# Where a one-number tile lies, and where all tiles behind it begin

## The chip, the core and the metric

The kernel runs on one core of one Trainium2 chip. Five engines work side by side: TensorE (PE in the profile, with its weight loads listed as PEld), VectorE (DVE), ScalarE (ACT), GpSimd (POOL) and SyncE (SP), which only starts transfers. The metric is the device time of one execution in microseconds. Three runs of the kernel before took 1090.83, 1091.79 and 1092.25 us; the median is 1091.79 us.

## The reference

One decoder block for 512 tokens of width 1024, in float32:

```
h     = rms_norm(x)
uv, z, xBC, dt, gates = split(h @ w_in)
y_a   = gelu(u) * (W_s @ layer_norm(gelu(v)) + b)     in 128-token chunks, W_s lower triangular
y_b   = rms_norm(ssd_scan(silu(conv(xBC)), dt) * silu(z))      32 heads, 8 groups, chunks of 128
x     = x + (sigmoid(ga) * (y_a @ w_proj_a) + sigmoid(gb) * (y_b @ w_proj_b)) @ w_out
x     = x + relu(rms_norm(x) @ w_mlp_up)**2 @ w_mlp_down
out   = rms_norm(x)
```

Nearly all of the arithmetic lies in the large products h @ w_in, the three projections and the two MLP products.

## The kernel before, in words

Every large product is made exact enough by splitting each factor in two parts of type float32r, a high part and the rest, and by adding three products: high by low, low by high, high by high. These are lines 132, 133 and 134 (`mm3`). TensorE takes two operands: a stationary one of 128 rows by 128 columns, which a weight load brings in, and a moving one of 128 rows and up to 512 columns, which streams past it. In the profile's names "acc<-hTl,whi" the moving operand is named first (hTl) and the stationary one second (whi).

The weights come as slabs of 128 x 1024 numbers. `Slabs` (lines 66 to 106) loads a slab from memory into `wraw`, ScalarE copies it into `whi`, and VectorE writes the rest to `wlo` (lines 91 and 92). Two orders of the product exist. `chan_major` (line 189) holds a weight part stationary and lets 512 tokens of the activations move past it: hT (the normalised input), yA, yB (the branches' outputs) and h2 (the second norm's output). `tok_major` (line 146) holds 128 tokens of the activations stationary and lets 512, or 352, weight columns move. The small products of the scan (lines 495, 573 to 575, 599, 601, 639) and the transposes (lines 225, 601, 658, against the unit matrix `ident`) are woven between the large ones by a list of due steps (`Weave`, line 111).

Order and waits come from the order of the code and from the tile framework. What matters here is where tiles lie. A pool is a stretch of each partition of the on-chip memory; pools opened on the left side follow one another in the order in which they are opened, and each tile in them begins at the next multiple of 32 bytes. The left side is opened as const, wpool, small, dtp, big, htp, and then pools that come and go behind these. One pool, mg, which holds the merged activations mh and ml of the output projection, is opened from the right end.

The tile in question is `mhalf` (line 285): the number -0.5 in each partition, 4 bytes, which POOL uses as the exponent of each inverse square root (lines 207, 473, 652). It lies in const, between `ident` and `triu`. Since it takes 32 bytes and not a multiple of 128, everything behind it starts 32 bytes past a multiple of 128; after the pool small, whose tiles add 1216 bytes, everything starts 96 past one.

Of the kernel before, what the change touches and what calls it, by code (L numbers as in the profile page):

```python
# [10 lines left out]
F32 = mybir.dt.float32  # L11
# [6 lines left out]
P = 128  # L18
T = 512
NT = T // P  # L20
DM = 1024
# [4 lines left out]
HD = 64  # L26
DFF = 4096
EPS = 1e-6
# steps (of three products of 512 columns) from a group's projection to the stages of its scan
SD, SA, SI, SS, SB, SC = 9, (12, 20), 8, 7, 9, 9  # L30
N2D = 8
WARM = 2, 0

# columns of the per-channel parameter tile
PV_CONVW, PV_CONVB, PV_BG, PV_SSMG = 0, 128, 160, 176
PV_N = 192
SL = 1024
# v's columns and dt's 32 go in three groups of 352, dt's first
VW = 352
NV = 12  # L40

# [2 lines left out]
def block_kernel(ctx: ExitStack, tc: tile.TileContext, x, w_v, w_all, wspt, pvec, hvec, g_mix, g_mlp, g_fin, v_g, v_b,  # L44
# [6 lines left out]
    const = ctx.enter_context(pool("const"))  # L51
# [10 lines left out]
    def sm_tile():  # L62
        return ps.tile([P, T], F32, tag="sm", name="sm", bufs=4)

# [1 line left out]
    class Slabs:  # L66
        def __init__(self):
            self.ready, self.raws, self.loaded, self.made = [], [], 0, 0
# [25 lines left out]
            self.made += 1  # L94

        def ahead(self, n):
            """Have n slabs in the making beyond those taken."""
            while len(self.ready) < n and self.made < self.n:
                self.make()

# [6 lines left out]

    slabs = Slabs()

# [1 line left out]
    class Weave:  # L111
        def __init__(self):
            self.now, self.due, self.seq = 0.0, [], 0
# [14 lines left out]
    wv = Weave()  # L128

    def mm3(o, st, mv, first, last, d=1.0):  # L130
        """o (+)= stationary.T @ moving, both as (hi, lo) parts"""
        nc.tensor.matmul(o, st[0], mv[1], start=first, stop=False)  # L132
        nc.tensor.matmul(o, st[1], mv[0], start=False, stop=False)  # L133
        nc.tensor.matmul(o, st[0], mv[0], start=False, stop=last)  # L134
        wv.step(d)
# [8 lines left out]
        return slice(t * P, (t + 1) * P)  # L144

    def tok_major(actT, evac, order="slabs", n=T, halve_last=False):
        """For n output columns: 4 token tiles, 4 slabs of two k-tiles with the weights moving."""
        accs = [acc_tile()[:, :n] for _ in range(NT)]

        def unit(t, kk, w):  # L150
            for j in range(2):
                k = 2 * kk + j
                mm3(accs[t], cut(actT, k, tsl(t)), wk(w, j, n), k == 0, k == KD - 1, n / T)

        if order == "slabs":
            for kk in range(4):
                w = slabs.take()
                for t in range(NT):
                    unit(t, kk, w)
                    if kk == 3:  # L160
                        evac(t, accs[t])
        else:
            # the last token tile by halves of the columns, for a shorter way out
            ws = [slabs.take(0)]
            last = [accs[-1][:, 0:256], sm_tile()[:, 0:256]] if halve_last else []

            def half(hf, kk):
                for j in range(2):
                    k = 2 * kk + j
                    w = cut(ws[kk], slice(j * T + hf * 256, j * T + (hf + 1) * 256))  # L170
                    mm3(last[hf], cut(actT, k, tsl(NT - 1)), w, k == 0, k == KD - 1, 0.5)

            slabs.ahead(2)
            for t in range(NT - len(last) // 2):
                unit(t, 0, ws[0])
            for hf in range(len(last)):
                half(hf, 0)
            ws += [slabs.take(0) for _ in range(3)]
            slabs.ahead(1)
            for t in range(NT - len(last) // 2):  # L180
                for kk in (1, 2, 3):
                    unit(t, kk, ws[kk])
                evac(t, accs[t])
            for hf in range(len(last)):
                for kk in (1, 2, 3):
                    half(hf, kk)
                evac(NT - 1, last[hf], hf)

    def chan_major(actT, evac, n=1, ahead=2):
        """n tiles of 128 output channels over all tokens, the weights stationary."""  # L190
        for i in range(n):
            w = slabs.take(ahead)
            acc = acc_tile()
            for k in range(KD):
                mm3(acc, wk(w, k), cut(actT, k), k == 0, k == KD - 1)
            evac(i, acc)

# [1 line left out]
    pv = const.tile([P, PV_N], F32, name="pv")  # L199
    hv = const.tile([P, 96], F32, name="hv")  # L200

    def rms_scale(ss):
        """(ss / DM + EPS) ** -0.5"""
        ms = small.tile([P, 1], F32, tag="rms_ms", name="rms_ms", bufs=4)
        nc.vector.tensor_scalar(ms, ss, 1.0 / DM, EPS, ALU.mult, ALU.add)  # L205
        rs = small.tile([P, 1], F32, tag="rms_rs", name="rms_rs", bufs=4)
        nc.gpsimd.tensor_tensor(rs, ms, mhalf, ALU.pow)  # L207
        return rs

    def rms_norm(xt, gs, work):  # L210
        """The 128 tokens of xt normalised over the free dim, times the gains gs (by halves)."""
        sq = work.tile([P, DM], F32, tag="rms_sq", name="rms_sq", bufs=1)
        ss = small.tile([P, 1], F32, tag="rms_ss", name="rms_ss", bufs=4)
        nc.scalar.activation(sq, xt, AF.Square, accum_out=ss)  # L214
        rs = rms_scale(ss)
        h = work.tile([P, DM], F32, tag="rms_h", name="rms_h", bufs=2)
        for b in range(2):
            hb = slice(b * T, (b + 1) * T)
            nc.vector.scalar_tensor_tensor(h[:, hb], xt[:, hb], rs, gs[b], ALU.mult, ALU.mult)  # L219
        return h  # L220
# [30 lines left out]
    gm = gm_cm.__enter__()  # L251
    v = gm.tile([P, NT, DM], F32, name="v")

# [1 line left out]
    ph0_cm = pool("ph0")  # L255
    ph0 = ph0_cm.__enter__()
    grow = ph0.tile([1, DM], F32, name="grow")
# [2 lines left out]
    with tc.manual_schedule():  # L260
# [11 lines left out]
        for i in range(2):  # L272
            for b in range(2):
# [8 lines left out]
        ident = const.tile([P, P], F32, name="ident")  # L282
        nc.gpsimd.affine_select(ident, ones, pattern=[[-1, P]], base=0, channel_multiplier=1,
                                compare_op=ALU.is_equal, fill=0.0)
        mhalf = const.tile([P, 1], F32, name="mhalf")
        nc.gpsimd.memset(mhalf, -0.5)
        # triu[s, l] = 1 where s <= l
        triu = const.tile([P, P], F32, name="triu")
        nc.gpsimd.affine_select(triu, ones, pattern=[[1, P]], base=0, channel_multiplier=-1,
                                compare_op=ALU.is_ge, fill=0.0)  # L290
# [32 lines left out]
            hs.append(h)  # L323

        def part(i, b, eng):
            """half a slab into its parts, the low one by eng"""
            if eng is None:
                nc.scalar.copy(parts[i][0][:, b], raws[i][:, b])
            else:
                eng.tensor_sub(parts[i][1][:, b], raws[i][:, b], parts[i][0][:, b].bitcast(F32))  # L330
# [69 lines left out]
                nc.scalar.activation(v[:, t, 0:VW - NH], accs[t][:, NH:VW], AF.Gelu)  # L400
                nc.vector.tensor_add(xr[:, t, :], accs[t][:, 0:NH], hv[:, 0:NH])

# [1 line left out]
    def dt_side():  # L404
        def softplus():
            # softplus(x) = max(x, 0) + log1p(exp(-|x|)); log1p(e) = 2 atanh(e / (2 + e))
            xf = flat(xr)
            ax, e, d, u, u2, q = (dtw.tile([P, NC], F32, name=f"dt_{i}") for i in range(6))
            nc.vector.scalar_tensor_tensor(ax, xf, -1.0, xf, ALU.mult, ALU.max)
# [38 lines left out]

    dt_side()

# [1 line left out]
    gm2_cm = pool("gm2")  # L452
    gm2 = gm2_cm.__enter__()
    wsp = gm2.tile([P, NG, P], F32, name="wsp")
# [61 lines left out]
    chan_major(yA, pa_evac, KD)  # L516
    ya_cm.__exit__(None, None, None)

# [1 line left out]
    ybp_cm = pool("ybp")  # L520
    ybp = ybp_cm.__enter__()
    yB = tuple(ybp.tile([P, KD, T], F32R, name=n) for n in ("yBh", "yBl"))
# [27 lines left out]
        return xc  # L550

    def ssd(g, xc, last_delay=None):
        """Weave the group's scan into the steps to come."""
        h0, h1 = R * g, R * (g + 1)
        st = {}

# [18 lines left out]
            nc.tensor.matmul(o, a[0], b[0], start=False, stop=True)  # L575

        def decay(hf):
            """exp(cs[l] - cs[s]) of two chunks, where s <= l"""
            lm = sd.tile([P, 2, R, P], F32, tag="lm", name="lm", bufs=2)
            for j in range(2):  # L580
                nc.sync.dma_start(lm[:, j], csd[2 * hf + j, h0:h1, :].partition_broadcast(P))
            lmf = lm.rearrange("p j r q -> p (j r q)")
            for j in range(2):
                for r in range(R):
                    nc.vector.tensor_scalar(lm[:, j, r, :], lm[:, j, r, :], ncs[:, 2 * hf + j, h0 + r:h0 + r + 1], None,
                                            ALU.add)
                st["lm", 2 * hf + j] = lm[:, j]
            nc.gpsimd.affine_select(lm, lm, pattern=[[0, 2], [0, R], [1, P]], base=0, channel_multiplier=-1,
                                    compare_op=ALU.is_ge, fill=-1e30)
            nc.scalar.activation(lmf, lmf, AF.Exp)  # L590
# [26 lines left out]
            st[c] = lm, xdt, xD  # L617

        def stage_s(c):
            """the state after chunk c"""  # L620
            hs = st.get("hs")
            stp = sm_tile()
            mm3s(stp[:, 0:256], *st["s", c])
# [60 lines left out]
        if g == 4:  # L684
            chan_major(yB, pb1_evac, KD)

# [1 line left out]
    def gb_evac(n, acc):  # L688
        sg = sd.tile([P, T], F32, tag="cv", name="sgb", bufs=2)
        nc.scalar.activation(sg, acc, AF.Sigmoid, bias=pv[:, PV_BG + KD + n:PV_BG + KD + n + 1])  # L690
# [30 lines left out]
    ybp_cm.__exit__(None, None, None)  # L721
    ht_cm.__exit__(None, None, None)
    tok_major(mg_t, res_evac(0))
    # the second half leads into the second norm, token tile by token tile
    n2 = ctx.enter_context(pool("n2"))
    gbc = n2.tile([P, DM], F32, name="gbc2")
    nc.sync.dma_start(gbc, g_mlp.partition_broadcast(P))
# [10 lines left out]

    mg_cm.__exit__(None, None, None)

# [1 line left out]
    mp_cm = pool("mlp")  # L742
    mp = mp_cm.__enter__()
    for qd in range(4):
# [57 lines left out]
    mp_cm.__exit__(None, None, None)  # L802


# [1 line left out]
def _stationary(w):  # L806
    """[K, N] -> [N / 128, 128 (k in tile), K]: one slab for 128 outputs over K = 1024"""
    k, n = w.shape
    return w.reshape(k // P, P, n // P, P).transpose(2, 1, 0, 3).reshape(n // P, P, k)


def _moving(w):
    """[K, N] -> [N / 512, K / 256, 128 (k in tile), 1024]: slabs of two k-tiles for 512 outputs"""
    k, n = w.shape
    return w.reshape(k // 256, 2, P, n // T, T).transpose(3, 0, 2, 1, 4).reshape(n // T, k // 256, P, SL)

# [52 lines left out]
```

## Time and profile before

| what | value |
|---|---|
| median of three runs | 1091.79 us |
| the profiled execution, first to last instruction (span) | 1088.7 us |
| PE busy, and its loads (PEld) | 1076.5 us (99%), 896.0 us (82%) |
| DVE, ACT, POOL busy | 612.6, 439.3, 137.3 us |
| mean granted TensorE clock | 0.998 |

The runs' times hold about 3 us that lie around the span. A PE at 99% is always at work by this measure, but the measure doesn't tell at what pace: the profile models the ends of matmuls, and one lasts longer than the distance from its start to the next start. The pace is read from the starts.

### The profile page before, as it was taken

To read this page: it belongs to the slowest core of one execution; us is meant where nothing else is said; L and a number is where in the kernel's file an instruction comes from. 1 tells how busy PE (TensorE), PEld (TensorE's weight loads), DVE (VectorE), ACT (ScalarE), POOL (GpSimd) and SP (SyncE) were. 2 spreads that over 40 slices of the span, in tenths; PEclk is the share of its full clock that TensorE was granted. 3 is DMA by queue.
4 is the path that set the end of the run, shared out by engine and by line. 5 is a ranking of instruction groups with operands and counts; after the bars stand their busy time and mean duration, and the time that the engine had idled before them with its cause. 6 is when DMAs were issued, how large, how long until landed. Compare 5 with 4: busy or idle time off the path is not lost. (4 is left out here: it accounts for less than half of the span.)

```text
span 1088.7 us, 13415 instructions
## 1 busy us (share of the span) xinstructions
PE 1076.5 (99%) x5205; PEld 896.0 (82%) x5205; DVE 612.6 (56%) x1040; ACT 439.3 (40%) x666; POOL 137.3 (13%) x188
## 2 busy tenths in 40 slices
PE   8999999999999999999999999999999999999997
PEld 7988888888888888888887888889888888888886
DVE  4672444346887895647778865364344434433443
ACT  5643333334556456444565532244213313312332
POOL 3020000001432432301324300000000000000000
PEclk9999999999999999999999999999999999999999
DMA  6433224232333333332323233513233232233222
GB/s 210 140 124 102 78 80 135 96 97 78 98 98 116 98 97 116 98 97 93 101 78 98 78 97 115 195 61 115 97 97 96 93 95 86 95 97 97 97 78 78
DMA packets 34626, 111.32 MB, mean 102 GB/s; under 512 B 3970, under 2 KB 4738, under 8 KB 34563
## 3 DMA queue, kind: packets, MB, share of 16 engines
q1 hardware_dynamic: 34560, 110.46, 31.9%
q8 instruction: 41, 0.67, 0.2%
q14 instruction: 23, 0.18, 0.1%
q10 hardware_dynamic: 2, 0.00, 0.0%
HBM read 108.29 MB, written 2.16 MB: 101 GB/s over the span
## 5 line engine op out<-in xcount | busy, mean ns | idle before, releaser
L92 DVE TENSOR_TENSOR wlo<-wraw,whi 128x1024 fp32r<-128x1024 f32 (+1 forms) x178 | 214.9, 1208 | 179.5 <-ACT whi L91 179.3
L91 ACT CAST whi<-wraw 128x1024 fp32r<-128x1024 f32 (+1 forms) x178 | 183.2, 1030 | 227.8 <-PE acc L134 210.8
L132 PE MATMUL acc<-hTl,whi 128*128 128x512 f32 x448 | 181.8, 406 | 0.0
L133 PE MATMUL acc<-hTh,wlo 128*128 128x512 f32 x448 | 176.9, 395 | 0.0
L134 PE MATMUL acc<-hTh,whi 128*128 128x512 f32 x448 | 176.8, 395 | 0.0
L132 PE MATMUL acc<-h2l,whi 128*128 128x512 f32 (+1 forms) x288 | 106.6, 370 | 0.2 <-DVE h2l L229 0.2
L134 PE MATMUL acc<-h2h,whi 128*128 128x512 f32 (+1 forms) x288 | 106.3, 369 | 0.0
L133 PE MATMUL acc<-h2h,wlo 128*128 128x512 f32 (+1 forms) x288 | 106.3, 369 | 0.0
L134 PEld LDWEIGHTS acc<-hTh,whi 128*128 128x128 f32 x448 | 84.0, 188 | 20.5
L134 PE MATMUL acc<-whi,ah 128*128 128x512 f32 (+1 forms) x256 | 99.9, 390 | 0.0
L133 PE MATMUL acc<-whi,al 128*128 128x512 f32 (+1 forms) x256 | 99.4, 388 | 0.0
L132 PE MATMUL acc<-wlo,ah 128*128 128x512 f32 (+1 forms) x256 | 98.5, 385 | 0.0
L132 PEld LDWEIGHTS acc<-hTl,whi 128*128 128x128 f32 x448 | 84.3, 188 | 17.1
L133 PEld LDWEIGHTS acc<-hTh,wlo 128*128 128x128 f32 x448 | 84.3, 188 | 17.1
L545 DVE SCALAR_TENSOR_TENSOR cv<-acc,pv,cv 128x511 f32<-128x511 f32 (+2 forms) x96 | 71.5, 745 | 31.8 <-ACT cv L543 31.1
L132 PE MATMUL acc<-wlo,hTh 128*128 128x512 f32 (+1 forms) x208 | 78.0, 375 | 0.1
L133 PE MATMUL acc<-whi,hTl 128*128 128x512 f32 (+1 forms) x208 | 76.0, 366 | 0.0
L134 PE MATMUL acc<-whi,hTh 128*128 128x512 f32 (+1 forms) x208 | 75.8, 366 | 0.0
L750 DVE TENSOR_TENSOR relu<-relu 128x512 f32<-128x512 f32 x32 | 22.2, 693 | 89.8 <-ACT relu L749 89.8
L207 POOL TENSOR_TENSOR rms_rs<-rms_ms,mhalf 128x1 f32<-128x1 f32 x12 | 6.6, 550 | 458.4 <-DVE rms_ms L205 458.4
L749 ACT ACTIVATE relu<-acc 128x512 f32<-128x512 f32 x32 | 19.2, 599 | 111.5 <-PE acc L134 111.5
L132 PEld LDWEIGHTS acc<-h2l,whi 128*128 128x128 f32 x288 | 54.1, 188 | 10.7 <-DVE h2l L229 0.6
(202 smaller groups left out, 1848.9 us busy)
## 6 DMA issues: line engine op xcount, KB each, us to landing
wraw<-in_w_all SPq DMA_DIRECT2D x168, 512.0 KB, 3.5
lm<-csd SPq DMA_DIRECT2D x32, 256.0 KB, 4.3
wraw<-in_w_v SPq DMA_DIRECT2D x10, 352.0 KB, 3.3
x<-in_x SPq DMA_DIRECT2D x4, 512.0 KB, 5.4
out<-rms_h SPq DMA_DIRECT2D x8, 256.0 KB, 2.1
xt<-in_x SPq DMA_DIRECT2D x3, 512.0 KB, 6.2
wraw<-in_w_v SPq DMA_DIRECT2D x4, 176.0 KB, 5.3
xt<-in_x SPq DMA_DIRECT2D x2, 256.0 KB, 3.3
```

The source lines that it names most:

```text
L91: nc.scalar.copy(hi, raw)
L92: nc.vector.tensor_sub(lo, raw, hi.bitcast(F32))
L132: nc.tensor.matmul(o, st[0], mv[1], start=first, stop=False)
L133: nc.tensor.matmul(o, st[1], mv[0], start=False, stop=False)
L134: nc.tensor.matmul(o, st[0], mv[0], start=False, stop=last)
L207: nc.gpsimd.tensor_tensor(rs, ms, mhalf, ALU.pow)
L545: nc.vector.scalar_tensor_tensor(cv[:, s_:], acc[:, :T - s_], cw[:, 3 - s_:4 - s_], cv[:, s_:], ALU.mult, ALU.add)
L749: nc.scalar.activation(r_, acc, AF.Relu)
L750: nc.vector.tensor_mul(r_, r_, r_)
```

## The change

`mhalf` leaves const for small, where it is given 16 numbers (64 bytes) of which the first is used. All other edits are removed comments and shifted line numbers. As built, the instructions of each engine, their order and their waits are the same as before; only addresses differ.

```diff
-        mhalf = const.tile([P, 1], F32, name="mhalf")
+
+        mhalf = small.tile([P, 16], F32, name="mhalf")[:, 0:1]
         nc.gpsimd.memset(mhalf, -0.5)
```

In the built programs the tiles that TensorE reads begin at these distances past a multiple of 128 bytes (a slice of such a tile starts at a multiple of 128 from the tile's own start):

| tiles | role | before | after |
|---|---|---|---|
| ident, ones | both roles in small products | 0 | 0 |
| triu | stationary, one product | 32 | 0 |
| whi, wlo | stationary in chan_major, moving in tok_major | 32 | 0 |
| hT, yA, yB, h2 (high and low) | moving in chan_major, hT stationary in tok_major too | 96 | 0 |
| ah, al (the MLP's activations) | stationary in tok_major | 96 | 0 |
| v, wsp, xc, lm, xdt, bT, cT, xdd2, hs2, yg, rms_h | the small products | 96 | 0 |
| mh, ml | stationary in the output projection | 96 | 96 |

## Rows read from the trace of the kernel before

**Rows 1.** The page, part 1: busy time, share of the span, instructions.
```profile
span 1088.7 us, 13415 instructions
PE 1076.5 (99%) x5205; PEld 896.0 (82%) x5205; DVE 612.6 (56%) x1040; ACT 439.3 (40%) x666; POOL 137.3 (13%) x188
```

**Rows 2.** Waits of PE: engine, line, waited for, us in total, times, longest.
```profile
PE sm L658 <- DVE yg L653: 2.3, 2, 1.8
PE acc L296 <- POOL mhalf L286: 1.4, 1, 1.4
PE sm L225 <- DVE rms_h L322: 1.3, 2, 1.0
```

**Rows 3.** Groups of PE's matmuls by shape: count, busy us, mean ns, idle before.
```profile
L132 PE MATMUL acc<-hTl,whi 128*128 128x512 f32 x448 | 181.8, 406 | 0.0
...
L132 PE MATMUL acc<-wlo,ah 128*128 128x512 f32 x248 | 96.3, 388 | 0.0
...
L132 PE MATMUL acc<-h2l,whi 128*128 128x512 f32 x224 | 88.6, 395 | 0.0
...
L132 PE MATMUL acc<-wlo,hTh 128*128 128x512 f32 x128 | 52.1, 407 | 0.1
L132 PE MATMUL acc<-yBl,whi 128*128 128x512 f32 x128 | 51.3, 401 | 0.0
...
L132 PE MATMUL acc<-wlo,hTh 128*128 128x352 f32 x80 | 25.9, 324 | 0.0
...
L132 PE MATMUL acc<-wlo,mh 128*128 128x512 f32 x64 | 25.3, 395 | 0.0
L132 PE MATMUL acc<-yal,whi 128*128 128x512 f32 x64 | 25.2, 394 | 0.0
...
L132 PE MATMUL acc<-h2l,whi 128*128 128x256 f32 x64 | 18.0, 281 | 0.2 <-DVE h2l L229 0.2
```

**Rows 4.** PE in order of time, chan_major at 816 us: start us, us, what.
```profile
816.00 0.39 PE L134 MATMUL acc<-h2h,whi 128*128 128x512 f32 x1
...
818.80 0.39 PE L134 MATMUL acc<-h2h,whi 128*128 128x512 f32 x1
```

**Rows 5.** The same view, tok_major at 776 us.
```profile
775.71 0.39 PE L132 MATMUL acc<-wlo,ah 128*128 128x512 f32 x1
...
778.46 0.39 PE L132 MATMUL acc<-wlo,ah 128*128 128x512 f32 x1
```

**Rows 6.** The same view, 352 columns at 40 us.
```profile
39.76 0.32 PE L134 MATMUL acc<-whi,hTh 128*128 128x352 f32 x1
...
43.12 0.32 PE L134 MATMUL acc<-whi,hTh 128*128 128x352 f32 x1
```

**Rows 7.** The same view: transposes against ident, and 256-column products, at 729 to 735 us.
```profile
728.79 0.28 PE L132 MATMUL acc<-h2l,whi 128*128 128x256 f32 x1
...
730.91 0.28 PE L132 MATMUL acc<-h2l,whi 128*128 128x256 f32 x1
...
731.97 1.04 PE L225 MATMUL sm<-ident,rms_h 128*128 128x128 f32 x8
...
733.20 0.28 PE L132 MATMUL acc<-h2l,whi 128*128 128x256 f32 x1
...
734.56 0.28 PE L132 MATMUL acc<-h2l,whi 128*128 128x256 f32 x1
```

**Rows 8.** The same view, small products whose operands both lie 96 past.
```profile
306.09 0.28 PE L573 MATMUL sm<-xdd2l,bTh 128*128 128x256 f32 x1
...
306.45 0.40 PE L132 MATMUL acc<-wlo,hTh 128*128 128x512 f32 x1
```

**Rows 9.** Busy time by stretch: engines, granted clock, DMA share, GB/s.
```profile
560.00:640.00 80.00, 78.25 (x413) 65.72 (x413) 68.47 (x141) 40.32 (x71) 26.65 (x35) 1.00 0.28 81
730.00:1088.00 358.00, 351.93 (x1635) 290.65 (x1633) 147.03 (x181) 106.43 (x149) 2.19 (x4) 1.00 0.30 95
```

**Rows 10.** POOL's inverse square roots, which read mhalf: duration min/median/max, first and last.
```profile
L207 POOL TENSOR_TENSOR rms_rs<-rms_ms,mhalf x12: 548/550/557, 6.0 to 1083.8; 128x1 f32<-128x1 f32 x12
```

## The prediction

> **What bounds the kernel now.** I read the busy shares first, then TensorE's waits, then its groups by shape, and then single starts in order of time. The shares show PE busy for 1076.5 of 1088.7 us, with the next engine at 56% [rows 1]. The waits show that PE stands still for somebody else during 2.3 + 1.4 + 1.3 us [rows 2], and 0.2 us more before h2's first product [rows 3]: 5.2 us in all. So there is no wait to take away: the time is the number of products times the distance between their starts, and only that distance can change it much. It has to be read from starts, since the modelled duration of a 512-column product (388 to 407 ns, [rows 3]) overlaps its successor.
>
> The distances: with activations moving, twelve 512-column products take from 816.00 to 818.80 us, 233.3 ns each [rows 4]. With weights moving, twelve take from 775.71 to 778.46 us, 229.2 ns each [rows 5]. With 352 columns, 21 products (seven rounds of three) take from 39.76 to 43.12 us, 160.0 ns each [rows 6]. The granted clock is 1.00 from 730 us on [rows 9] and 0.998 over the span: the upper level, 2.4 GHz. A column per clock would make 213.3 ns of 512 columns and 146.7 of 352. That a column costs about a clock can be seen: 160 more columns cost 69.2 ns, 0.43 ns each. So each product carries an excess of 20.0, 15.9 or 13.3 ns, and this excess is all that the change can work on.
>
> **The change part by part.** It adds and removes no instruction, transfer or wait; the orders are the same. What it does to POOL is nothing I can price: the inverse square root still reads one number per partition, 550 ns [rows 10]. VectorE, ScalarE and the transfers also get other addresses. I cost that at nothing, because PE covers them: over the last 358 us DVE works 147 of them [rows 9]. Where that cover is thin, at 560 to 640 us (DVE 68.5 of 80 us), a faster PE will wait for DVE more than the 1.75 us that it does now; below I take 2 us off for that.
>
> What is left is the pace of PE. Products whose operands move from 32 or 96 past a multiple of 128 bytes to 0, each count three times that of its row since lines 133 and 134 repeat it [rows 3]:
> - activations moving, 512 columns: 448 + 224 + 128 + 64 = 864 per line, 2592 in all, at 233.3 ns: 604.7 us;
> - weights moving, 512 columns: 248 + 128 = 376 per line, 1128 in all, 229.2 ns: 258.5 us;
> - the output projection, 64 x 3 = 192, whose moving operand moves to 0 while the stationary mh and ml stay at 96;
> - 352 columns: 240, and 48 in the first stage, 160 ns: 46.1 us;
> - 256 columns: 192 of h2 and 48 at the end.
>
> Does the start matter at all? The trace has no 512-column product with a moving operand at a multiple of 128, so its price has to be bounded. What it does have is a pair that differs in the offsets and little else: moving at 96 with stationary at 32 has 20.0 ns of excess, moving at 32 with stationary at 96 has 15.9 [rows 4, 5]. The order of the three products, the loads and the columns are alike. So I take it that offsets count for some nanoseconds.
> - The best end: the excess falls to what the only aligned moving operand shows. Eight transposes move ident past rms_h; their last start is 1.04 - 0.27 us after the first, 110 ns apart, 3 ns over the 106.7 that 128 columns take at 1.2 GHz (how I read the pace of the load that bounds them) [rows 7]. With 3 ns left per product: 2592 x 17.0 = 44.1, 1128 x 12.9 = 14.6, 192 x 12.9 = 2.5, 288 x 10.3 = 3.0, and about 1 for the 256-column ones: 65 us.
> - A middle mark: the excess falls only to the least that a large product shows. Durations run about 162 ns above distances (395 [rows 3] against 233.3 [rows 4] in h2), so the group at 388 stands at 226 [rows 3], an excess of 12.7. That gives 2592 x 7.3 + 1320 x 3.2 = 23 us.
> - The worst end: two streams that begin at the same offset collide more, priced with the rivals at 34 us more.
>
> I forecast between the first two marks, since alignment should take away what comes of straddling but hardly all that a load beside the stream costs: (65 + 23) / 2 = 44 us, less 2 us for DVE: 42. Against the profiled execution that is 1088.7 - 42 = 1046.7 us of span. Its runs stand 3.1 us above it (1091.79 - 1088.7, start and end around the span, which nothing here touches): 1050 us.
>
> One rule speaks against any gain. The excess exists at offsets 32 and 96 [rows 4, 5], both multiples of 16. The Trainium skill (SBUF — State Buffer, Specifications) has memory lines of 16 bytes and wants only two hits in a line; its section Operand start alignment asks only for a multiple of the element size, adding "This is about legality, not speed". By that rule nothing changes, which is the second rival; the 4 ns between rows 4 and 5 don't fit it well.
>
> **The rivals.**
> - *The whole excess goes.* For it: the only aligned row stands near its floor. Against: that row moves 128 columns, not 512. 65 us less: 1027 us.
> - *Nothing changes.* Both offsets may be good enough already, and the difference between rows 4 and 5 may come of something else that goes with the roles of the operands, such as the tile's place. 1091.8 us.
> - *Only the worse offset is cured.* Activations fall to the pace of weights: 2592 x 4.1 = 10.6 us, 1081 us. For it: the pair of rows 4 and 5 taken literally.
> - *Slower.* The load of the next stationary operand and the moving stream run at once. Today they lie 64 bytes apart modulo 128; afterwards they begin at the same offset everywhere. Products where both already lie at 96 take 0.36 us for three, 120 ns per 256 columns [rows 8], against 113.3 for h2's at 96 and 32 (twelve from 733.20 to 734.56 us [rows 7]): 6.7 ns more. Against it: the same h2 products ran at 117.8 ns a little earlier (18 from 728.79 to 730.91 [rows 7]) with the same addresses, so that pace also depends on how the two streams fall in time; and the three of rows 8 stand alone between other forms. If it is real and each large product with its one load pays it once: 3720 x 6.7 = 25 us, 1117; if in proportion to columns, twice that, 50 us. I take 34 us: 1126. It decides as soon as collisions cost more per product than straddling gives back.
> - A rule bears on the slower case. What the rows show is an excess of 13 to 20 ns in products with one load each. The Trainium skill (TensorE: Matmul & The Clock Gate, Step-by-step: what each phase is for) says that TensorE has two independent read ports and that loading the next weights "doesn't steal SBUF read bandwidth from the running matmul". By it the slower case could not be, and the time would be one of the others; the two paces of the same 256-column products, 113.3 and 117.8 ns, speak against so clean a separation.
> - *The change doesn't reach all it says:* mh and ml stay at 96. If the stationary operand's offset is what counts, the 192 products of the output projection keep 229 ns; that is under 3 us and decides nothing.
>
> **How the numbers follow.** Chances: the forecast of about 1050 (1034 to 1072) 0.33; the whole excess, 1022 to 1034, 0.20; only the worse offset cured, 1072 to 1089, 0.13; nothing 0.17; slower 0.17. Differences under 0.2%, about 2 us, can't be told from none. So faster 0.66, same 0.17, slower 0.17. The range has to hold 0.8: from 1024 to 1094 it leaves out the slower case and a sliver below. The likeliest case's own range is 1034 to 1072.
>
> **What would show it.** Right: 512-column starts near 221 ns in place of 233 and 229, both orders at one pace, durations in the groups down by as much, unchanged counts, and PE waiting a little more for DVE at 560 to 640 us. If the output projection's products (line 132, wlo by mh) lag behind the MLP's, the stationary offset counts as well; if they keep pace, the moving one alone does. Starts at 233 and 229 as before show that nothing changed. Wrong altogether: starts beyond 236 ns, or a time that grows while the starts shrink, because another engine became late.

## The result, and the profile after

The kernel after takes 1076.97 us (median of four runs, 1076.60 to 1077.32) against 1091.83 us (four runs, 1090.83 to 1092.25) before: a ratio of 0.9865 with a 95% interval of 0.9851 to 0.9879, 14.9 us less. I had forecast 42 us less. The direction came out, and the size is about a third of what I said. The time lies in the wide range (1024 to 1094), but not in that of the likeliest case (1034 to 1072). The profiled execution is 13.8 us shorter in span.

The page of the kernel after, part 1, which answers to [rows 1]:

```profile
span 1074.9 us, 13415 instructions
PE 1062.4 (99%) x5205; PEld 897.2 (83%) x5205; DVE 612.8 (57%) x1040; ACT 439.5 (41%) x666; POOL 137.5 (13%) x188
```

All counts are the same, PE is again busy for 99%, and its busy time falls by 14.1 us, about as much as the span. So the same products run closer together. The waits of PE after, answering to [rows 2]:

```profile
PE sm L659 <- DVE yg L654: 2.6, 3, 1.6
PE acc L297 <- POOL mhalf L287: 1.4, 1, 1.4
PE sm L225 <- DVE rms_h L323: 0.6, 2, 0.4
PE sm L574 <- DVE xdd2l L570: 0.4, 2, 0.2
PE sm L303 <- DMA grow<-in_g_mix: 0.3, 1, 0.3
```

They add up to 5.3 us, about the 5.2 of before: the wait for rms_h is 0.7 us shorter, the 0.2 us before h2's first product is gone, and the last two lines are new. PE's groups after, answering to [rows 3] (count, busy us, mean ns, idle before):

```profile
L132 PE MATMUL acc<-hTl,whi 128*128 128x512 f32 x448 | 179.8, 401 | 0.0
...
L132 PE MATMUL acc<-wlo,ah 128*128 128x512 f32 x248 | 96.5, 389 | 0.0
...
L132 PE MATMUL acc<-h2l,whi 128*128 128x512 f32 x224 | 87.1, 389 | 0.0
...
L132 PE MATMUL acc<-wlo,hTh 128*128 128x352 f32 x80 | 25.9, 324 | 0.0
L132 PE MATMUL acc<-wlo,mh 128*128 128x512 f32 x64 | 25.4, 398 | 0.0
...
L132 PE MATMUL acc<-h2l,whi 128*128 128x256 f32 x64 | 18.4, 287 | 0.0
```

Three things stand here. The groups with activations moving fall by 5 to 6 ns (hT 406 to 401, h2 395 to 389). The 352-column group stays at 324. And two groups last clearly longer: the output projection (mh, 395 to 398) and the 256-column products (281 to 287). These are modelled durations: wlo by ah goes from 388 to 389, although its starts come closer. The distances between starts say it more sharply. PE in order of time, after, with activations moving (start us, us, what; the stage of [rows 4]), with weights moving (the stage of [rows 5]) and with 256 columns [rows 7]:

```profile
721.15 0.28 PE L132 MATMUL acc<-h2l,whi 128*128 128x256 f32 x1
...
722.96 0.28 PE L132 MATMUL acc<-h2l,whi 128*128 128x256 f32 x1
...
759.62 0.39 PE L134 MATMUL acc<-h2h,whi 128*128 128x512 f32 x1
...
762.34 0.39 PE L134 MATMUL acc<-h2h,whi 128*128 128x512 f32 x1
...
803.82 0.39 PE L134 MATMUL acc<-whi,ah 128*128 128x512 f32 x1
...
806.54 0.39 PE L134 MATMUL acc<-whi,ah 128*128 128x512 f32 x1
```

The 512-column pairs are twelve products apart: 2.72 us / 12 = 226.7 ns for both orders, where before it was 233.3 and 229.2. The 256-column pair is fifteen apart: 1.81 / 15 = 120.7 ns (119.9 over all 174 undisturbed distances), where it was 113.3 to 117.8 before, 114.1 on average. At 2.4 GHz (the granted clock was 0.999 over the span) 226.7 ns are 544 clocks for 512 columns, 160.0 ns are 384 for 352, and 119.9 are 288 for 256: after the change every large product but those of the output projection costs its columns plus 32 clocks, 13.3 ns, in the steady stages, whatever its width.

Where the 13.6 us between the first and the last matmul went, by summing all distances between starts, kind by kind: hT moving (1344 products) 318.8 to 312.2, h2 moving (672) 156.8 to 152.4, yB (384) 90.3 to 88.0, yA (192) 44.8 to 43.5, together -14.5 us; the MLP's activations stationary 170.3 to 168.7 and hT stationary 90.5 to 90.2, together -1.9; 352 columns -0.1; against it 256 columns +1.3, the output projection +0.7, and the transposes of yg, with their waits, +0.8. The sum is -13.7 us; the small products left out make up the rest.

### The profile page after: what moved, and what is told of

Read it like the earlier page. It is cut to its first block, busy times and chain, and to the rows that moved or that the text cites. A ratio compares the mean times of both kernels' runs of the same rounds, so it can differ in the third digit from the quotient of the medians.

```text
span 1074.9 us, 13415 instructions
## 1 busy us (share of the span) xinstructions
PE 1062.4 (99%) x5205; PEld 897.2 (83%) x5205; DVE 612.8 (57%) x1040; ACT 439.5 (41%) x666; POOL 137.5 (13%) x188
## 4 chain that ended last, share of the span: by engine, by line
PE 81%; DVE 10%; POOL 3%; issue 2%; ACT 2%; DMA 1%; POOLq 0%; SPq 0%; ACTq 0%
PE acc L132 25%; PE acc L134 25%; PE acc L133 25%; DVE cv L546 3%; DVE lm L586 1%; DVE wlo L92 1%; POOL xD L644 1%; PE sm L640 1%; POOL lm L589 1%; POOL yrs L653 1%; DMA lm<-csd 1%; PE sm L496 1%; PE sm L225 1%; PE acc L339 1%; DVE yg L654 1%
## 5 line engine op out<-in xcount | busy, mean ns | idle before, releaser
L133 PE MATMUL acc<-hTh,wlo 128*128 128x512 f32 x448 | 174.6, 390 | 0.0
```

## The experiments

The alignment theory (A), as the change has it: operands have to begin at a multiple of 128 bytes. Its rival, the distance theory, formed from the two groups that became slower: what counts is the distance between the beginnings of the stationary and the moving operand, not where either begins. In the first four runs (moved; both alike at 32; roles exchanged; mh and ml at a multiple of 128) this distance was still counted modulo 128, and their expectations say so; what these runs showed made it 256. A third, the load theory (L), was on what remains: the 32 clocks are the price of the weight load, in proportion to its columns. All edits are against the kernel after. Offsets are given in bytes modulo 256, weights first, then activations: 32 and 224 before, 0 and 0 after. "Distance" (D) is stationary minus moving, modulo 256, so that the two orders of the product have opposite distances (before: 64 with activations moving, 192 with weights moving). From here on "distance" alone means this one, in bytes. A pace is a time: the mean over undisturbed distances between starts, of 512-column products where no other width is named.

**Moved, not padded** (weights 0, activations 224).

```diff
-        mhalf = small.tile([P, 16], F32, name="mhalf")[:, 0:1]
+        mhalf = small.tile([P, 1], F32, name="mhalf")[:, 0:1]
```

> Only the move, without the padding to 64 bytes: the weight parts begin at 0, the activations stay at 96. Theory A (only operands that both begin at a multiple of 128 run at 226.7 ns): activations-moving products at about 233 ns, weights-moving ones at the 233 ns that the output projection shows in the changed kernel with this pair of offsets, so 1092 to 1097 us, nothing gained or a little lost. Theory B (what counts is that both begin at the same offset modulo 128): the same. Theory C (the stationary operand's offset alone counts): activations-moving at 226.7, weights-moving at 233, about 1079 us. Theory D (the moving operand's alone): the reverse, about 1089 us.

Measured: 1096.43 us (1095.64 to 1097.01), ratio 1.0045 [1.0032, 1.0058], slower than before. Activations moving 233.3 ns as before, weights moving 233.3 instead of 229. So half of the change, which brings the weights to a multiple of 128, gains nothing and loses some. The two theories that one operand's start alone counts (C and D in the expectation) fall; alignment and distance had forecast the same here. PE's groups of this kernel:

```profile
L133 PE MATMUL acc<-whi,al 128*128 128x512 f32 x248 | 98.1, 395 | 0.0
...
L133 PE MATMUL acc<-h2h,wlo 128*128 128x512 f32 x224 | 88.7, 396 | 0.0
```

**Both alike, but 32 past a multiple of 128** (32 and 32).

```diff
-        triu = const.tile([P, P], F32, name="triu")
+        triu = const.tile([P, P + 8], F32, name="triu")[:, 0:P]
```

> The changed kernel with 32 bytes more in the pool of constants: weight parts and activations all begin 32 past a multiple of 128, so no large operand is aligned but both share one offset. Theory A (multiples of 128 are what counts): starts at 229 to 236 ns, 1088 to 1100 us. Theory B (the difference of the two offsets counts, and zero is good): 226.7 ns in both orders and 1077 us, the output projection at 229 as in the kernel before.

Measured: 1076.61 us, ratio 0.9858 [0.9836, 0.9881], the same as after. The groups of this kernel are those of after:

```profile
L132 PE MATMUL acc<-wlo,ah 128*128 128x512 f32 x248 | 96.5, 389 | 0.0
...
L132 PE MATMUL acc<-h2l,whi 128*128 128x512 f32 x224 | 87.1, 389 | 0.0
```

and so are its starts; PE in order of time, h2 moving, twelve products:

```profile
815.71 0.39 PE L132 MATMUL acc<-h2l,whi 128*128 128x512 f32 x1
...
818.43 0.39 PE L132 MATMUL acc<-h2l,whi 128*128 128x512 f32 x1
```

2.72 us / 12 = 226.7 ns. The output projection, whose distance is 192 here as in the kernel before, is back at 229.0 ns. None of the weight parts and activations that PE reads begins at a multiple of 128 here, the weights are where they were before, and the whole gain is there. The alignment theory falls by this run.

**Activations at a multiple of 128, 128 bytes off the weights** (0 and 128).

```diff
-        mhalf = small.tile([P, 16], F32, name="mhalf")[:, 0:1]
+        mhalf = small.tile([P, 48], F32, name="mhalf")[:, 0:1]
```

> All activations 128 bytes further on than in the changed kernel: every large operand at a multiple of 128, D = 128 modulo 512 with activations moving and 384 with weights moving. Theory A (multiples of 128 are what counts) and B128: 226.7 ns everywhere, 1077 us. Theory B256 (the two must begin at the same offset modulo 256): about 232 ns, as the output projection ran in the run with mh and ml at a multiple of 128 (D there 128), so 1089 to 1096 us.

Measured: 1095.40 us, ratio 1.0034 [1.0021, 1.0047]. Every large operand but mh and ml begins at a multiple of 128, as in the kernel after, and it is slower than before. PE in order of time, h2 moving, twelve products:

```profile
829.79 0.40 PE L133 MATMUL acc<-h2h,wlo 128*128 128x512 f32 x1
...
832.58 0.39 PE L133 MATMUL acc<-h2h,wlo 128*128 128x512 f32 x1
```

2.79 us / 12 = 232.5 ns. Beside the run before, this is the same from the other side: aligned and slow, unaligned and fast. It also rules out a distance counted modulo 128, by which 128 would be as good as 0.

**256 bytes off the weights** (activations moved by 256: 0 and 0 again).

```diff
-        mhalf = small.tile([P, 16], F32, name="mhalf")[:, 0:1]
+        mhalf = small.tile([P, 80], F32, name="mhalf")[:, 0:1]
```

> All activations 256 bytes further on than in the changed kernel, so that every operand still begins at a multiple of 128 (mh and ml at 96 as before), and stationary and moving now begin at the same offset modulo 512 (the difference D was 256). Theory B128 (D counts modulo 128) and B256 (modulo 256): 226.7 ns everywhere, 1077 us. Theory B512 (D counts modulo 512, 256 being a good place): another pace, 229 to 236 ns, 1086 to 1097 us, or a better one below 226.

Measured: 1077.20 us, ratio 0.9869 [0.985, 0.9889], both orders at 226.7 ns. PE in order of time, h2 moving, twelve products (226.7 ns):

```profile
816.01 0.39 PE L132 MATMUL acc<-h2l,whi 128*128 128x512 f32 x1
...
818.73 0.39 PE L132 MATMUL acc<-h2l,whi 128*128 128x512 f32 x1
```

So 256 bytes of distance are as good as none.

**192 off** (0 and 192: the distances 64 and 192 of the kernel before, at other places).

```diff
-        mhalf = small.tile([P, 16], F32, name="mhalf")[:, 0:1]
+        mhalf = small.tile([P, 64], F32, name="mhalf")[:, 0:1]
```

> All activations 192 bytes further on than in the changed kernel: D (where the stationary operand begins minus where the moving one does) is 64 with activations moving and 448, that is 192 modulo 256, with weights moving. Theory B256 (only D modulo 256 counts): the kernel before in every group, whose D were 320 and 192: 233.3 and 229 ns, 114 ns for 256 columns, 1091 us. If D counts modulo 512 with two good places (0 and 256): other paces than before in the activations-moving products.

Measured: 1093.47 us, ratio 1.0024 [1.0013, 1.0035]; 233.3 ns with activations moving, 228.9 with the MLP's activations stationary. PE in order of time, h2 moving, twelve products (233.3 ns):

```profile
825.75 0.40 PE L134 MATMUL acc<-h2h,whi 128*128 128x512 f32 x1
...
828.55 0.40 PE L134 MATMUL acc<-h2h,whi 128*128 128x512 f32 x1
```

These paces of before come back, though no large operand but mh and ml lies where it lay. The total is 2.6 us above before. Of the 2.0 us by which the profiled span is longer, 0.7 lie in the output projection, whose distance is 224 here (233.3 ns) and was 192 before (229.0), and 0.7 in h2's 256-column products: I had expected 114 ns for them, and they run at 117.8 throughout, where before they ran at 113.3 for the most part.

**Roles exchanged** (64 and 128: distance 192 with activations moving, 64 with weights moving).

```diff
-        mhalf = small.tile([P, 16], F32, name="mhalf")[:, 0:1]
+        mhalf = small.tile([P, 32], F32, name="mhalf")[:, 0:1]
...
-        triu = const.tile([P, P], F32, name="triu")
+        triu = const.tile([P, P + 16], F32, name="triu")[:, 0:P]
```

> Weight parts at 64, activations at 0: every operand at a multiple of 64, the difference 64 as in the kernel before. Theory A with 64 in place of 128: 226.7 ns, 1077 us. Theory A with 128: between, the order whose moving operand is at 0 faster. Theory B: the pace of the kernel before, 233.3 and 229, 1091 us.

Measured: 1088.95 us, ratio 0.9981 [0.997, 0.9991]. Weights moving now take 233.3 ns everywhere, and activations moving take 229 in hT, yB and yA: the two paces of before have changed places with the distance, so they never belonged to the roles. With the distance modulo 128 I had expected them where they were before; 64 and 192 have to be told apart. One thing doesn't fit: h2, the same tile throughout, runs at 228.9 ns in the first and third quarter of the MLP and at 233.3 in the second and fourth. At this distance there are two paces. PE in order of time, second and third quarter (13 and 12 products):

```profile
815.76 0.40 PE L132 MATMUL acc<-h2l,whi 128*128 128x512 f32 x1
...
818.80 0.40 PE L133 MATMUL acc<-h2h,wlo 128*128 128x512 f32 x1
...
904.62 0.39 PE L132 MATMUL acc<-h2l,whi 128*128 128x512 f32 x1
...
907.37 0.39 PE L132 MATMUL acc<-h2l,whi 128*128 128x512 f32 x1
```

3.04 / 13 = 233.8 and 2.75 / 12 = 229.2 ns.

**160 off** (0 and 160: distances 96 and 160).

```diff
-        mhalf = small.tile([P, 16], F32, name="mhalf")[:, 0:1]
+        mhalf = small.tile([P, 56], F32, name="mhalf")[:, 0:1]
```

> All activations 160 bytes further on: D modulo 256 is 96 with activations moving and 160 with weights moving, the two places that no run has had for a large group. Theory B256: neither is better than 226.7 ns; I expect 229 to 235 ns in both, 1088 to 1097 us. If one of them is under 226.7, another place would be the best.

Measured: 1100.17 us (1099.84 to 1100.49), ratio 1.008 [1.0051, 1.011], the slowest of all; 234.3 ns with activations moving, 233.4 with weights moving, and about 163 for 352 columns, the only run where these left 160 by more than 1 ns. PE's groups of this kernel:

```profile
L133 PE MATMUL acc<-whi,al 128*128 128x512 f32 x248 | 98.9, 399 | 0.0
...
L133 PE MATMUL acc<-h2h,wlo 128*128 128x512 f32 x224 | 88.8, 396 | 0.0
```

**The output projection alone, at a multiple of 128** (mh and ml at 128, all else as after).

```diff
-    mg_t = tuple(mg.tile([P, KD, T], F32R, name=n) for n in ("mh", "ml"))
+    mg_t = (mg.tile([P, KD, T], F32R, name="mh"),
+            mg.tile([P, KD * T + 24], F32R, name="ml")[:, 0:KD * T].rearrange("p (k t) -> p k t", k=KD))
```

> The changed kernel with 96 bytes behind ml, so that mh and ml begin at a multiple of 128 too. Theories A and B alike: the 192 products of the output projection fall from 233-236 to 226.7 ns, 1.3 to 1.7 us less: 1075.5 us. If the output projection is slow for another reason (its place at the right end): 1077 us.

Measured: 1075.54 us, ratio 0.9853 [0.9835, 0.9872]. The projection's groups of this kernel:

```profile
L132 PE MATMUL acc<-wlo,mh 128*128 128x512 f32 x64 | 25.4, 398 | 0.0
L133 PE MATMUL acc<-whi,ml 128*128 128x512 f32 x64 | 25.3, 395 | 0.0
```

They are as in the kernel after, where mh begins at 224: 395 to 398 ns, and from starts 232.3 against 233.3 ns. Moving them to a multiple of 128 did next to nothing for them. Alignment and the distance modulo 128 had both forecast 226.7 here, and both missed. The 1.4 us by which this median is lower lie within the intervals of the two ratios.

**The output projection alone, alike with the weights** (mh and ml at 0). The same edit with 120 in place of 24.

```diff
...
+            mg.tile([P, KD * T + 120], F32R, name="ml")[:, 0:KD * T].rearrange("p (k t) -> p k t", k=KD))
```

> The changed kernel with 480 bytes behind ml, so that mh and ml too begin at D = 256 from the weight parts. Theories B256 and B512: the 192 products of the output projection fall from 233 to 226.7 ns, 1.2 us off the changed kernel's 1077.0: 1075.7 us. Theory B128 (which the run with 96 bytes behind ml speaks against): no change to that run, 232 ns there.

Measured: 1075.70 us (1075.16 to 1076.35), ratio 0.9855 [0.9838, 0.9871]. The projection's groups of this kernel:

```profile
L132 PE MATMUL acc<-wlo,mh 128*128 128x512 f32 x64 | 25.1, 392 | 0.0
L133 PE MATMUL acc<-whi,ml 128*128 128x512 f32 x64 | 24.9, 389 | 0.0
```

Its steady pace is 226.7 ns against 233.3 in the kernel after: with 192 products that is 1.3 us. The pace shows the gain; the totals of this version and of the one after can't be told apart. It is the version I would keep.

**Fewer columns loaded.**

```diff
-    def chan_major(actT, evac, n=1, ahead=2):
+    def chan_major(actT, evac, n=1, ahead=2, m=P):
...
-                mm3(acc, wk(w, k), cut(actT, k), k == 0, k == KD - 1)
+                c = P if k in (0, KD - 1) else m
+                mm3(acc[0:c], cut(w, slice(k * P, k * P + c)), cut(actT, k), k == 0, k == KD - 1)
...
-            chan_major(h2T, up_evac, KD)
+            chan_major(h2T, up_evac, KD, m={1: 64, 2: 32, 3: P}[qd])
```

> The changed kernel, whose MLP up-products load only 64 of the 128 stationary columns in the second quarter and 32 in the third for six of their eight steps (k = 1 to 6); the other 64 or 96 output channels miss those steps, so the output is not the reference's. Theory L (the 32 clocks of excess left per product are what one load of 128 columns takes from the moving stream): 16 and 8 clocks, starts 220.0 and 216.7 ns apart in those steps against 226.7 in the last quarter. Theory S (a fixed cost of each product's start or of its moving stream): 226.7 ns in all three.

Measured: one run, 1079.01 us. The loads become shorter in this kernel:

```profile
L133 PEld LDWEIGHTS acc<-h2h,wlo 128*128 128x128 f32 x192 | 36.3, 189 | 5.0
...
L133 PEld LDWEIGHTS acc<-h2h,wlo 128*64 128x64 f32 x48 | 6.5, 134 | 4.5
...
L133 PEld LDWEIGHTS acc<-h2h,wlo 128*32 128x32 f32 x48 | 5.2, 109 | 5.8
```

but the products do not come closer; PE's groups of this kernel:

```profile
L133 PE MATMUL acc<-h2h,wlo 128*128 128x512 f32 x128 | 49.8, 389 | 0.0
...
L133 PE MATMUL acc<-h2h,wlo 128*32 128x512 f32 x48 | 18.9, 394 | 0.0
L133 PE MATMUL acc<-h2h,wlo 128*64 128x512 f32 x48 | 18.9, 394 | 0.0
```

The stage with 64 columns (a quarter of its products still load 128) runs at 229.2 ns, that with 32 at 230.6, and the same stage with 128 at 226.7. Among the products with the shorter loads alone it is 230.0 and 231.6. The load theory wants the excess to fall to a half and a quarter of 32 clocks, 220.0 and 216.7 ns; it grew. That theory falls, and what the 32 clocks are stays open.

Put together, the pace of 512 columns by distance:

| distance modulo 256 | ns | read in |
|---|---|---|
| 0 | 226.7 | after, both alike at 32, 256 off; mh when alike |
| 32 | 233.3 | moved, not padded |
| 64 | 233.3 | before, 192 off, roles exchanged |
| 96 | 234.3 | 160 off |
| 128 | 232.3 to 232.5 | 128 off, both orders; mh at a multiple of 128 |
| 160 | 233.4 | 160 off |
| 192 | 229 (and 233.3 in half of h2's stage, roles exchanged) | before, 192 off, roles exchanged; mh with both alike at 32 |
| 224 | 233.3 | moved, not padded; mh after |

The distance decides the pace of 512 columns in every run, but for the two paces at 192. Only multiples of 32 were tried, and why the distance matters, what the two operands share, is not shown. The change hits distance 0 by two shifts: leaving const moved the weights down by 32, and the 64 bytes in small, less those 32, moved the activations up by 32.

## Why the prediction was right or wrong

- *What bounds the kernel:* right. Counts, the sum of the waits and the other engines' busy times stayed; the distances between TensorE's starts gave nearly the whole difference (13.6 of 13.8 us of span).
- *"Offsets count for some nanoseconds", from the 4 ns between [rows 4] and [rows 5]:* right, and the rival "nothing changes" falls. The Trainium skill (SBUF — State Buffer, Specifications) has lines of 16 bytes; that rule alone would have left 1091.8, and starts that are all multiples of 32 gave 226.7 to 234.3 ns. Its section Operand start alignment speaks of legality only, and no run here contradicts that.
- *The step that failed:* "I forecast between the first two marks, since alignment should take away what comes of straddling but hardly all that a load beside the stream costs". There is no straddling to take away: unaligned operands at distance 0 have the whole gain and aligned ones at distance 128 have none. What the change removes is the cost of a wrong distance, 16 clocks (6.7 ns) with activations moving and about 6 with weights moving, and 32 clocks remain. The middle mark had nearly that pace, 226 ns, but by luck: it was read off the 388 ns of wlo by ah [rows 3] less 162 ns, and [rows 5] show the starts of that very group 229.2 ns apart. From there I went halfway to the 3 ns of the transposes [rows 7], so to about 8 ns of excess in place of 13.3; the transposes are another kind of product, and no group of 512-column products has under 13.3 ns of excess in any run.
- *Sizes:* activations moving gave 14.5 us, against 18.9 at the middle mark (2592 x 7.3) and 44.1 at the best end. In the steady stages it was 6.7 ns each (h2, yA), but hT's 1344 products gave only 4.9 ns on average, since the scan's small products break the rhythm in between: the first 192, with nothing woven in, gave 6.6 ns each, and the eight scan groups between 0.1 and 6.7. Weights moving gave 1.9 us for 1128, against 3.6 and 14.6.
- *Two terms had the wrong sign.* For the 256-column products I took about 1 us off; they cost 1.3 more. For the output projection I bounded the gain at 2.5 us and said it would keep 229 ns at worst; it went to 233.3, because the weights moved against mh, from distance 192 to 224; with the distance back at 192 (both alike at 32) it took 229.0.
- *The slower rival:* its price was right where I read it and its sign was wrong elsewhere. [rows 8] had both operands alike and 120 ns for 256 columns, and after the change all 256-column products take that. But 120 ns is 106.7 and 13.3 of excess, the same 13.3 as in [rows 6]; added to 512 columns' 213.3 it makes 226.7, a gain. I compared 120 with 113.3 and scaled the difference up, when the row's own excess was to be carried over. By that the sum would have been 2592 x 6.6 + 1128 x 2.5 - 192 x 6.7 = 18.6 us, 1073 us.
- *The rule of two read ports.* The pace depends on where the stationary operand begins against the moving one, by 7.6 ns between the best and the worst distance. The Trainium skill (TensorE: Matmul & The Clock Gate, Step-by-step: what each phase is for) says that loading doesn't take read bandwidth from the running product. These runs don't show what the two share, but they aren't independent of each other's address.
- *"Only the worse offset is cured", 1081:* near in time (its 1072 to 1089, given 0.13, hold the result), wrong in kind: both orders changed their pace, and to one below 229. That the stated range holds the time is owed to its width and to this rival, not to the mechanism.
- *DVE's 2 us:* not seen where I put them. Busy time by stretch, after, which answers to [rows 9]:

```profile
560.00:640.00 80.00, 78.26 (x411) 66.34 (x410) 67.33 (x137) 40.54 (x69) 24.71 (x32) 1.00 0.29 86
```

PE was busy for 78.25 of these 80 us before and is for 78.26: a TensorE 1.3% faster did not meet a late DVE there. Elsewhere in the scan a little of it shows: 0.4 us of new waits for xdd2l, and the 0.8 us of yg's transposes. The 3.1 us "around the span" were misread: in every run with a span on record the time is 1.7 us above that run's own span. The other 1.4 us lie between two executions, the profiled one and the median one.

## What to carry to other kernels

Where TensorE is always busy, read the distance between starts in clocks, take off the columns, and compare the rest between all pairs of tiles by the distance of their addresses, before assigning it to alignment. Here tiles that meet as stationary and moving operand in 512-column products want the same offset modulo 256 bytes, and padding a small tile that lies between their pools does that; one that lies in a third pool, as mh, has to be moved as well. A row in which both operands already stand as the change will put them is the price to use, carried over as an excess and not as a difference.

## What the runs showed of the hardware that I had not expected

- 512-column float32r products, each with its own load, come every 226.7 ns when stationary and moving operand begin alike modulo 256 bytes, and every 229 to 234.3 ns otherwise; over the kernel that is 1077 against up to 1100 us with the same instructions.
- The excess at distance 0 is the same 32 clocks at 256 and 512 columns, and shorter loads (134 and 109 ns instead of 189) didn't lower it.
- Narrow products order the distances otherwise: 256 columns took 119.9 ns at distance 0, but 113.3 or 117.8 at 64. The 352-column products took 160 in the kernels before and after alike; every second slice of their slabs begins 1408 bytes, which is 128 modulo 256, behind the first, so that their distances come in pairs, 64 and 192 before and 0 and 128 after, and nothing like the 6 ns that 512 columns lose at 128 shows. Why the same addresses give two paces, here and in half of h2's stage in the run with roles exchanged, is not settled.
